# A conv-FFN kernel in split fp32: operand stores close behind their split, on another engine's queue, and operands of the second half loaded a group ahead

## The chip, the cores and the metric

The kernel runs on one core of one Trainium2 chip. The metric is the device time of one execution in microseconds; the time before is the median of three runs, 2267.11 us (2266.05 to 2268.96). The core has a tensor engine (PE; its weight loads are listed as PEld), a vector engine (DVE), a scalar engine (ACT), a general engine (POOL) and a synchronisation engine (SP), each with an instruction queue of its own that runs in order. A DMA is issued by an instruction in one of these queues: while that instruction waits for its data, everything behind it in the queue waits too.

## The reference, cut to what matters

One layer (S = 2048 tokens, D = 1024, F = 2816): a gated linear attention mixer, and then a feed-forward block with a causal convolution over the tokens.

```python
h = rmsnorm(x, mix_norm_w)
x = x + gla_mixer(h, ...)            # q, k, v, r, gates; scan over chunks; @ w_out
h = rmsnorm(x, ffn_norm_w)
u = causal_dwconv(h @ w_up, conv_w, conv_b)      # 3 taps over the tokens
g, val = jnp.split(u, 2, axis=-1)
x = x + (jax.nn.silu(g) * val) @ w_down
return rmsnorm(x, final_norm_w)
```

## The kernel before

**Products.** All large products are done in fp32 by three passes: `split` writes the rounded high half of an operand on ScalarE (a cast, L183) and the low half, what is left, on VectorE (a subtraction, L184); `mm3p` (L176 to L178) then issues high x low, low x high and high x high into one accumulation. On top of that, 2 x 2 blocks are multiplied with seven products, named p1, p5, p6, p7, p4, p2 and p3 in the order in which they run. p1, p6, p7 and p4 of a column add up in one PSUM bank (`ua`), and after p1, p6 and p7 ScalarE copies its contents out (c1 and c2 at L1050, c3 at L1145) before the next of the four may write on. p5 and p3 share the bank `uc`; p2 has its own, `ub`.

**Stages.** The mixer is done in four passes over the token tiles, R, A, B and Y. Y adds w_out's product to x; the result x1 goes to DRAM (`x1d`, L742), is normalised (`rows`), and is transposed and scaled into the operand rows of the feed-forward block (`blocks`, L745 to L762). Of those, the tiles of the first 1024 tokens stay on the chip (`hb2`); those of the second 1024 go to DRAM (`h2f`, L762) through a ring of two tiles. Then `phase_u(s)` runs for the halves s = 0 and s = 1: eleven groups g of two columns f, and in each group 14 jobs (seven products times two columns; a job is 12 matmuls 512 wide, four contraction tiles in three passes). A group multiplies the operands h (`hop`, kept on the chip, 4 x 512 columns in high and low) with the columns of w_up, convolves, gates (`gated`: silu(g) * val, on VectorE), and stores the seven combinations of its result that the down projection needs (`ad`, L1079 to L1095): three straight from the product, four over tiles that POOL adds up (`as`). The down projection follows after s = 1.

**Operands h.** The seven operands of each quarter of a half (`prep_h2`: p1, p5, p7, p3, p6, p2, p4 in its own order) are made from the rows, split into a tile `h2p` (L183 and L184), and stored to DRAM (`hd`, L785); four quarters make a half. This is spread over time by `spread`: a step each Y1 = 2.8 us of the planner's clock in pass Y for the first half, and each U1 = 11 us in phase U of s = 0 for the second half, starting U0 = 20 us in. A step first issues the store of the step before (`store()` at its head), so the operands of a step are in `held` for a whole step. The first half has three h2p tiles in the ring, the second half one. `load_op(s, o)` (L846) brings operand o of half s back in four DMAs, one for a quarter, into `uh`, where each product has exactly one tile: the load for s = 1 overwrites the operand of s = 0, so it waits until PE has used that for the last time. It is issued for s = 1 at the jobs k = 0, 2, ... 12 of s = 1's first group.

**Order.** Instructions are written in the order of a planner's clock: every `mm3p` advances it by 0.227 us a matmul, and `later_do(us, fn)` puts work off until the clock has gone that much further. The framework then sets each engine's order from this, and resolves what waits for what. Weights of a column come in two halves (`ur_f_0`, `ur_f_1`, L1017, two DMAs each, on SP except in the first group), into a ring of four, a group ahead; POOL forms the sums that p5, p6 and p3 need (`us`, L1027 to L1045). The DMAs that SP issues therefore stand in one row: weight loads, `ad` stores, operand stores, row loads (L780) and operand loads.

## Time and profile before

| | |
|---|---|
| median of three runs | 2267.11 us |
| profiled execution, its own time | 2264.65 us |
| its span | 2262.9 us |
| granted TensorE clock, mean | 0.983 |
| last x1 store of pass Y issued | 944.1 us |
| phase U, s = 0, groups g0 to g10 | 918.6 to 1401.1 us |
| preparation of the second half's operands | 960.2 to 1273.6 us |
| phase U, s = 1 | from 1401.1 us |

The page gives busy times of the engines, the DMA queues, the chain of work that ended last, and groups of instructions. The number behind a stage in a table of windows is the time in which each engine was busy in it; the granted clock is the share of full speed that the throttle allowed. In lists of waits, an engine's idle time is put down to what ended it. The rows on which the prediction rests are shown there.

### The profile page before, as it was taken

The numbers are of one execution on the slowest core, as the hardware profiler recorded it, in microseconds if no ns is written. First come the engines' busy times: TensorE is split into PE (matmuls) and PEld (weight loads), VectorE is DVE, ScalarE is ACT, GpSimd is POOL, SyncE is SP. The second block draws the span as 40 slices with busy tenths as digits, with TensorE's granted clock in tenths as the row PEclk, the third lists the DMA queues.
The fourth block names the chain that finished last, engine by engine and source line by source line (L and its number), as shares of the span: only waits on it lengthen the run. The fifth ranks groups of instructions, "written<-read, shape, count | busy, mean of one in ns | idle before, by whom it ended". The sixth has DMA issues, their size and how long they took to land.

```text
span 2262.9 us, 29154 instructions
## 1 busy us (share of the span) xinstructions
PE 2132.6 (94%) x9948; PEld 1744.8 (77%) x9948; DVE 1612.6 (71%) x2175; ACT 1109.8 (49%) x2020; POOL 698.5 (31%) x602
## 2 busy tenths in 40 slices
PE   5999989989997998889989999899999999999998
PEld 3888778877886886767777788788888888888886
DVE  7755787788778764388778777577777786557554
ACT  4554755565556675444454444344454543332343
POOL 1000111111111000254545565455555544035100
PEclk9999999999999999999999999999999999999999
DMA  6545684368457798934543437624233368454443
GB/s 220 191 163 182 215 280 133 124 207 307 158 162 232 265 330 307 327 125 139 171 146 126 140 98 258 209 73 124 86 117 94 112 229 324 136 186 158 140 166 118
DMA packets 301045, 411.77 MB, mean 182 GB/s; under 512 B 23246, under 2 KB 159614, under 8 KB 300896
## 3 DMA queue, kind: packets, MB, share of 16 engines
q1 hardware_dynamic: 270476, 362.45, 47.9%
q10 hardware_dynamic: 30420, 47.46, 6.4%
q8 instruction: 78, 1.28, 0.2%
q14 instruction: 71, 0.58, 0.1%
HBM read 266.70 MB, written 143.13 MB: 181 GB/s over the span
## 4 chain that ended last, share of the span: by engine, by line
PE 65%; DVE 12%; DMA 10%; ACT 5%; issue 4%; POOL 3%; SPq 1%; ACTq 0%; DVEq 0%; POOLq 0%
PE ua L176 5%; PE ua L177 5%; PE ua L178 5%; PE pd_p L177 5%; PE pd_p L178 5%; PE pd_p L176 5%; PE uc L178 3%; PE uc L176 3%; PE uc L177 3%; PE mp_R L176 2%; DVE t L1068 2%; PE mp_R L177 2%; PE mp_R L178 2%; PE mp_Y L176 2%; DMA hd_p<-h2p_p 2%
## 5 line engine op out<-in xcount | busy, mean ns | idle before, releaser
L176 PE MATMUL ua<-h_p,uw_p 128*128 128x512 f32 x704 | 284.3, 404 | 42.5 <-ACT c L1145 31.9
L177 PE MATMUL ua<-h_p,uw_p 128*128 128x512 f32 x704 | 282.3, 401 | 0.0
L178 PE MATMUL ua<-h_p,uw_p 128*128 128x512 f32 x704 | 281.8, 400 | 0.0
L1068 DVE SCALAR_TENSOR_TENSOR t<-u,cw,t 128x1024 f32<-128x1024 f32 x176 | 250.9, 1427 | 13.2 <-ACT t L1066 12.4
L177 PE MATMUL pd_p<-dw_p,da 128*128 128x512 f32 x616 | 239.7, 389 | 0.8 <-DVE da L184 0.8
L176 PE MATMUL pd_p<-dw_p,da 128*128 128x512 f32 x616 | 239.6, 389 | 0.0
L178 PE MATMUL pd_p<-dw_p,da 128*128 128x512 f32 x616 | 239.6, 389 | 0.0
L184 DVE TENSOR_TENSOR uw_p<-ur,uw_p 128x512 fp32r<-128x512 f32 x176 | 162.9, 940 | 64.8 <-ACT uw_p L183 56.8
L184 DVE TENSOR_TENSOR da<-da_p,da 128x512 fp32r<-128x512 f32 x154 | 135.4, 932 | 98.9 <-ACT da L183 98.8
L176 PEld LDWEIGHTS ua<-h_p,uw_p 128*128 128x128 f32 x704 | 136.2, 194 | 77.0 <-ACT c L1145 35.3
L183 ACT CAST da<-da_p 128x512 fp32r<-128x512 f32 x154 | 85.2, 619 | 201.7 <-PE pd_p L178 147.5
L178 PEld LDWEIGHTS ua<-h_p,uw_p 128*128 128x128 f32 x704 | 136.2, 194 | 30.9
L177 PEld LDWEIGHTS ua<-h_p,uw_p 128*128 128x128 f32 x704 | 136.7, 194 | 30.2
L184 DVE TENSOR_TENSOR uw_p<-us,uw_p 128x512 fp32r<-128x512 f32 x132 | 119.1, 909 | 56.5 <-ACT uw_p L183 55.2
L183 ACT CAST uw_p<-us 128x512 fp32r<-128x512 f32 x132 | 82.1, 622 | 137.2 <-POOL us L1030 87.4
L176 PE MATMUL uc<-h_p,uw_p 128*128 128x512 f32 x352 | 138.1, 392 | 0.0
L178 PE MATMUL uc<-h_p,uw_p 128*128 128x512 f32 x352 | 138.0, 392 | 0.0
L177 PE MATMUL uc<-h_p,uw_p 128*128 128x512 f32 x352 | 138.0, 392 | 0.0
L1066 ACT ACTIVATE t<-u,cw 128x1024 f32<-128x1024 f32 x88 | 109.7, 1247 | 53.8 <-DVE u L1158 53.8
L177 PEld LDWEIGHTS pd_p<-dw_p,da 128*128 128x128 f32 x616 | 115.6, 188 | 25.2 <-DVE da L184 1.3
L176 PEld LDWEIGHTS pd_p<-dw_p,da 128*128 128x128 f32 x616 | 115.6, 188 | 24.2
L178 PEld LDWEIGHTS pd_p<-dw_p,da 128*128 128x128 f32 x616 | 115.6, 188 | 23.8
(251 smaller groups left out, 5427.5 us busy)
## 6 DMA issues: line engine op xcount, KB each, us to landing
ur<-in_ffn_w_up_dram SPq DMA_DIRECT2D x168, 256.0 KB, 3.4
da_p<-ad_p SPq DMA_DIRECT2D x154, 256.0 KB, 3.8
hd_p<-h2p_p SPq DMA_DIRECT2D x56, 512.0 KB, 3.2
h_p<-hd_p SPq DMA_DIRECT2D x56, 512.0 KB, 7.6
ad_p<-as_p SPq DMA_DIRECT2D x88, 256.0 KB, 2.2
ad_p<-t SPq DMA_DIRECT2D x66, 256.0 KB, 3.2
x<-in_x_dram SPq DMA_DIRECT2D x32, 512.0 KB, 4.8
ch<-in_ffn_w_down_dram SPq DMA_DIRECT2D x61, 256.0 KB, 4.8
```

The source lines that it names most:

```text
L176: nc.tensor.matmul(ps_ap, ah, bl, start=(first and i == 0), stop=False, **kw)
L177: nc.tensor.matmul(ps_ap, al, bh, start=False, stop=False, **kw)
L178: nc.tensor.matmul(ps_ap, ah, bh, start=False, stop=(last and i == len(pairs) - 1), **kw)
L183: nc.scalar.copy(hi, src)
L184: nc.vector.tensor_sub(lo, src, f32(hi))
L1066: nc.scalar.activation(t, u[:, 2:2 + TS], AF.Identity, scale=cw[:, 2, c:c + 1], bias=cw[:, 3, c:c + 1])
L1068: nc.vector.scalar_tensor_tensor(t, u[:, k:k + TS], cw[:, k, c:c + 1], t, op0=ALU.mult, op1=ALU.add)
```

## The change

Six edits, all in where and when DMAs are issued:

- the rows of the second half go to DRAM from `cp_tile`, the ring of four that the evictions c1 and c2 use, instead of a ring of two of their own;
- the first half's h2p ring is four tiles instead of three;
- a step's operand store is issued `HLY` = 1.5 us (first half) or 3.0 us (second half) of the planner's clock behind its split, not at the head of the next step, and the second half's on ScalarE's queue;
- the x1 stores of the last two tiles are on ScalarE's queue;
- the second half's preparation starts 14 us into phase U, not 20;
- operand o of s = 1 is loaded in the last group of s = 0, directly behind the second column's job of the same product, and not in s = 1's first group.

```diff
-    Y0, Y1, U0, U1 = 3.0, 2.8, 20.0, 11.0
+    Y0, Y1, U0, U1 = 3.0, 2.8, 14.0, 11.0
+    HLY = (1.5, 3.0)
...
-               lambda name: p.tile([P, 2, 512], F32R, tag="h2p", name=name, bufs=3))
+               lambda name: p.tile([P, 2, 512], F32R, tag="h2p", name=name, bufs=4))
...
-        nc.sync.dma_start(x1d[t], xt)
+        (nc.scalar if t + 2 >= NTT else nc.sync).dma_start(x1d[t], xt)
...
-            t = hb2_tile(f"hb2_{tt}_{k}", tt < TT)
+            t = hb2_tile(f"hb2_{tt}_{k}") if tt < TT else cp_tile(f"hb3_{tt}_{k}")
...
-    def hb2_tile(name, kept):
-        return yp["p"].tile([P, 512], F32, tag="hb2" if kept else "hb3", name=name, bufs=10 if kept else 2)
+    def hb2_tile(name):
+        return yp["p"].tile([P, 512], F32, tag="hb2", name=name, bufs=10)
...
                 o, hl = held.pop()
-                nc.sync.dma_start(hd[s, o, j], f32(hl))
+                (nc.scalar if s else nc.sync).dma_start(hd[s, o, j], f32(hl))
...
             held.append((o, hl))
+            later_do(HLY[s], store)
...
-            if s > 0 and k == 0:
-                need(*(f"h2p{jj}" for jj in range(PAIRS, 2 * PAIRS)))
-            if s > 0 and k < 2 * len(OPS) and k % 2 == 0:
-                load_op(s, OPS[k // 2])
...
+            if s + 1 < NS and g == NQ - 1 and f % 2 == 1:
+                need(*(f"h2p{jj}" for jj in range(PAIRS, 2 * PAIRS)))
+                load_op(s + 1, o)
+            if o == "p3":
```

Line numbers of the changed kernel are one or two higher from L183 on (L184 is the cast, L786 the operand store, L848 the operand load, L1019 the weight load, L1052 and L1143 the evictions).

Three places show how the rows move. The first is ScalarE at products p6 and p7 of the group of columns 8 and 9 (s = 0). `uw` are weight halves being cast, `c_0_8` and `c_0_9` the evictions, `h2p` the operand step. Before:

```order
L183 CAST uw_9_p_11081<-ur_9_1_10818 128x512
L183 CAST uw_8_p_11098<-ur_8_1_10815 128x512
L1050 COPY c_0_8_11096<-ua_8_11003 128x512
L183 CAST uw_9_p_11115<-ur_9_1_10818 128x512
L1050 COPY c_0_9_11113<-ua_9_11022 128x512
L183 CAST uw_8_p_11146<-us_8_10907 128x512
L1145 COPY c_0_8_11135<-ua_8_11003 128x512
L183 CAST uw_9_p_11166<-us_9_10933 128x512
L183 CAST h2p_p_11453<-h2r_0_11433 128x512
L1145 COPY c_0_9_11161<-ua_9_11022 128x512
```

and now:

```order
L184 CAST uw_8_p_11103<-ur_8_1_10821 128x512
L786 DMA hd_p_2_328<-h2p_p_11596 128x1024
L1052 COPY c_0_8_11101<-ua_8_11008 128x512
L184 CAST uw_9_p_11121<-ur_9_1_10824 128x512
L184 CAST h2p_p_11718<-h2r_2_11402 128x512
L786 DMA hd_p_2_340<-h2p_p_11718 128x1024
L1052 COPY c_0_9_11119<-ua_9_11027 128x512
L184 CAST uw_8_p_11147<-us_8_10913 128x512
L1143 COPY c_0_8_11136<-ua_8_11008 128x512
L184 CAST uw_9_p_11167<-us_9_10934 128x512
L184 CAST h2p_p_11801<-h2r_0_11398 128x512
L786 DMA hd_p_2_324<-h2p_p_11801 128x1024
```

Three operand stores stand among the evictions where none stood, two of them directly ahead of a c2, and two casts of h2p steps stand here that stood elsewhere in the group.

The second is SP's queue at the boundary of the halves, where `ur_0` to `ur_3` are weights of s = 1, `ad_p_9` and `ad_p_10` stores of the last two groups of s = 0, and h_p<-hd_p the operand loads for s = 1. Before:

```order
L1017 DMA ur_0_0_13198<-in_ffn_w_up_dram 128x4x128 x2
L1079 DMA ad_p_9_351<-t_18_12880 512x1x128
L846 DMA h_p_13210<-hd_p_0_314 128x2x512
L1017 DMA ur_1_0_13201<-in_ffn_w_up_dram 128x4x128 x2
L1082 DMA ad_p_9_406<-t_19_12906 512x1x128
L1083 DMA ad_p_9_395<-t_19_12906 512x1x128
L1095 DMA ad_p_9_362<-as_9_p_12914 128x512
L1095 DMA ad_p_9_373<-as_9_p_12917 128x512
L1095 DMA ad_p_9_417<-as_9_p_12920 128x512
L1095 DMA ad_p_9_384<-as_9_p_12923 128x512
L1017 DMA ur_0_1_13204<-in_ffn_w_up_dram 128x4x128 x2
L1017 DMA ur_1_1_13207<-in_ffn_w_up_dram 128x4x128 x2
```

and now, one group later in the program:

```order
L848 DMA h_p_13206<-hd_p_2_340 128x2x512
L848 DMA h_p_13206<-hd_p_3_341 128x2x512
L1084 DMA ad_p_10_407<-t_21_13213 512x1x128
L1085 DMA ad_p_10_396<-t_21_13213 512x1x128
L1097 DMA ad_p_10_363<-as_10_p_13221 128x512
L1097 DMA ad_p_10_374<-as_10_p_13224 128x512
L1097 DMA ad_p_10_418<-as_10_p_13227 128x512
L1097 DMA ad_p_10_385<-as_10_p_13230 128x512
L1019 DMA ur_1_0_13236<-in_ffn_w_up_dram 128x4x128 x2
L1019 DMA ur_0_1_13239<-in_ffn_w_up_dram 128x4x128 x2
L1019 DMA ur_1_1_13242<-in_ffn_w_up_dram 128x4x128 x2
L1019 DMA ur_2_0_13305<-in_ffn_w_up_dram 128x4x128 x2
```

The weights ur_1_0, ur_0_1 and ur_1_1 stood ahead of group 9's last stores or right behind them, and stand now behind those of group 10 and behind the 28 operand loads; only ur_0_0 has kept its place.

The third is ScalarE at the end of pass Y, where x_14 and x_15 are the last two x1 tiles, and hb_14 rows on their way to DRAM. Now:

```order
L743 DMA x1d_92<-x_14_9221 128x1024
L203 ACTIVATE h_14_9613,ssq_d_9614<-x_14_9221 128x1024
L184 CAST uw_1_p_9676<-us_1_9674 128x512
L746 ACTIVATE h_14_9613<-x_14_9221,rstd_d_9618 128x1024
L743 DMA x1d_93<-x_15_9223 128x1024
L203 ACTIVATE h_15_9640,ssq_d_9641<-x_15_9223 128x1024
L1052 COPY c_0_0_9672<-ua_0_9659 128x512
L746 ACTIVATE h_15_9640<-x_15_9223,rstd_d_9645 128x1024
L759 ACTIVATE hb_14_0_9688<-pt_d_0_9683,nw_506 128x128 x4
```

Before, the two x1 stores stood on SP's queue, among the operand loads of s = 0:

```order
L846 DMA h_p_9606<-hd_p_3_309 128x2x512
L742 DMA x1d_92<-x_14_9221 128x1024
L846 DMA h_p_9633<-hd_p_0_310 128x2x512
L846 DMA h_p_9633<-hd_p_1_311 128x2x512
L846 DMA h_p_9633<-hd_p_2_312 128x2x512
L846 DMA h_p_9633<-hd_p_3_313 128x2x512
L742 DMA x1d_93<-x_15_9223 128x1024
```

Both have moved from behind those loads to just behind the sums that make their tiles.

## Prediction

> **What bounds the kernel now.** I read the page first, then a table of windows by stage, then the waits in those windows, and last the timeline around one stall. The page:

> ```profile
> span 2262.9 us, 29154 instructions
> PE 2132.6 (94%) x9948; PEld 1744.8 (77%) x9948; DVE 1612.6 (71%) x2175; ACT 1109.8 (49%) x2020; POOL 698.5 (31%) x602
> ```

> TensorE is busy 94% of the span, so what the change can win is idle time of PE, and the slow clock behind it. The windows (start:end, length, then busy time of PE, PEld, DVE, ACT, POOL, then granted clock, DMA share, GB/s) show where that is: the end of pass Y, gate/value groups g0 (from 918.6), g1 (from 972), g2 to g7, then g8 to g10, and s = 1's g0.

> ```profile
> 840.00:918.60 78.60, 68.52 (x306) 54.95 (x305) 38.03 (x63) 43.79 (x97) 9.26 (x11) 0.96 0.92 318
> 972.00:1018.00 46.00, 38.61 (x153) 30.57 (x153) 38.73 (x39) 22.73 (x36) 24.20 (x22) 0.93 0.44 143
> 1018.00:1285.80 267.80, 242.36 (x1002) 195.23 (x1001) 213.72 (x216) 125.02 (x191) 132.69 (x120) 0.95 0.44 144
> 1285.80:1401.10 115.30, 115.30 (x504) 94.22 (x503) 84.56 (x91) 57.00 (x85) 73.71 (x61) 1.00 0.51 163
> 1401.10:1449.30 48.20, 42.31 (x172) 34.05 (x171) 29.43 (x32) 19.15 (x29) 22.37 (x19) 0.93 0.71 244
> ```

> In g8 to g10, where the preparation of the second half is over, PE has no gap: 115.3/3 = 38.4 us a group, 2.74 a job of its 14. With the preparation a group takes 267.8/6 = 44.6. Against 38.4, g1 loses 7.6 and g2 to g7 lose 37.2, **44.8 us** together. s = 1's first group loses 48.2 - 38.4 = **9.8**. At the end of Y PE is idle 10.1 of 78.6 us.

> The waits of 972 to 1286 (who, for whom, total, times, longest) say what the 44.8 is:

> ```profile
> ACT h2p_p L183 <- DMA hd_p<-h2p_p: 56.1, 19, 8.3
> PE ua L176 <- ACT c L1145: 28.2, 7, 5.2
> ```

> and the timeline of one of them (start, duration, engine, line; in brackets the idle time before) shows it link by link, SP and ACT and PE:

> ```profile
> 1075.63 5.43 SPq L1095 DMA_DIRECT2D ad_p<-as_p  x4
> 1081.15 2.09 SPq L1017 DMA_DIRECT2D ur<-in_ffn_w_up_dram  x4
> 1083.29 0.49 SPq L785 DMA_DIRECT2D hd_p<-h2p_p  x1
> 1089.73 0.62 ACT L183 CAST h2p_p<-h2r 128x512 fp32r<-128x512 f32 x1 [8.29 <-DMA hd_p<-h2p_p]
> 1090.26 0.58 ACT L1145 COPY c<-ua 128x512 f32<-128x512 f32 x1
> 1090.89 0.79 PE L176 MATMUL ua<-h_p,uw_p 128*128 128x512 f32 x1 [5.20 <-ACT c L1145]
> ```

> The operand store waits on SP's queue behind four ad stores and four weight loads, the next cast waits on ScalarE until that store has landed (one h2p tile), the eviction of p7 stands behind the cast, and p4 waits 5.20 us for it. After it the clock drops (windows of PE's timeline, the granted clock third from the end, and the two matmuls that ended shorter stalls in pass Y):

> ```profile
> 1091.00:1094.00 3.00, 3.00 (x8) 2.38 (x9) 2.44 (x5) 2.50 (x4) 0.58 (x1) 0.52 0.68 223
> 853.61 0.50 PE L176 MATMUL mp_Y<-w_Y_p,h_Y_p 128*128 128x512 f32 x1 [2.58 <-ACT h_Y_p L183]
> 853.50:857.00 3.50, 3.16 (x9) 2.29 (x10) 2.58 (x4) 2.20 (x7) 0.00 (x0) 0.71 0.73 215
> 857.00:860.00 3.00, 3.00 (x12) 2.41 (x11) 0.34 (x1) 0.34 (x1) 0.00 (x0) 0.77 1.05 410
> 878.57 0.50 PE L176 MATMUL mp_Y<-w_Y_p,h_Y_p 128*128 128x512 f32 x1 [1.70 <-ACT h_Y_p L183]
> 878.50:881.00 2.50, 2.21 (x8) 1.61 (x9) 2.14 (x4) 2.14 (x7) 0.00 (x0) 1.00 0.56 151
> ```

> Three us at 0.52 cost about 1.5. The two windows from 853.5 follow a stall of 2.58 us, and lose (1 - 0.71) x 3.5 + (1 - 0.77) x 3 = 1.7; the stall of 1.70 lost nothing.

> **Term A, the end of Y.** Rows to DRAM from a ring of four, x1 stores of the last two tiles on ScalarE. The waits of 840 to 960:

> ```profile
> ACT hb L758 <- DMA h2f<-hb: 8.2, 2, 5.1
> PE mp_Y L176 <- ACT h_Y_p L183: 8.4, 3, 4.1
> ACT uw_p L183 <- DMA x1d<-x: 10.1, 1, 10.1
> PE ua L176 <- ACT c L1145: 3.8, 1, 3.8
> ```

> ScalarE waits twice for the ring of two; of PE's three waits for the operand rows, 8.4 - 1.7 = 6.7 us come from that. It waits 10.1 us for an x1 store that SP issued only behind the h_p loads, and PE 3.8 of it. With 1.7 of clock behind each of three stalls the whole is 6.7 + 3.8 + 5.1 = 15.6. But the DMA engines are 0.92 busy in 840:918.6: the h_p loads of s = 0 go at their pace, and PE that comes earlier waits for them. The larger ring also is one that g0's first evictions use, so those now wait for a row store. I count half of the ring's part (6.7 + 3.4)/2 = 5 and two thirds of the x1 part (3.8 + 1.7), 3.6: **-8.6**. Bounds: -3.8 (the x1 wait alone) and -15.6.

> **Term B, stores on ScalarE's queue behind their split.** SP's part of the stall goes: the store no longer waits for ad stores and weights. Its cost is the issue on ScalarE, 0.33 us as the h2f store takes there, 28 times, beside an engine busy 125.02 of 267.8; nothing unless something waits. What it brings is a wait: the store needs the low half, which VectorE subtracts late, and ScalarE queues behind it.

> In the timeline of ScalarE, VectorE and POOL, and among the page's DMA issues:

> ```profile
> 935.32 0.33 ACTq L762 DMA_DIRECT2D h2f<-hb  x1
> 1106.26 0.39 PE L176 MATMUL ua<-h_p,uw_p 128*128 128x512 f32 x1
> 1108.57 0.62 ACT L183 CAST h2p_p<-h2r 128x512 fp32r<-128x512 f32 x1 [0.38 <-DMA hd_p<-h2p_p]
> 1090.39 0.69 DVE L184 TENSOR_TENSOR h2p_p<-h2r,h2p_p 128x512 fp32r<-128x512 f32 x1 [7.32 <-ACT h2p_p L183]
> 1119.14 1.79 DVE L184 TENSOR_TENSOR h2p_p<-h2r,h2p_p 128x512 fp32r<-128x512 f32 x1
> 1120.85 3.48 DVE L184 TENSOR_TENSOR uw_p<-ur,uw_p 128x512 fp32r<-128x512 f32 x2
> 1118.70 1.67 POOL L1089 TENSOR_TENSOR as_p<-t,t 128x512 f32<-128x512 f32 x1 [1.18 <-DVE t L1075]
> hd_p<-h2p_p SPq DMA_DIRECT2D x56, 512.0 KB, 3.2
> ```

> The cast of 1108.57 had its subtraction end only at 1120.93: VectorE was busy with the convolution and the gating product, then took 1.74 to 1.79 a subtraction beside POOL's adds. By the order of the changed kernel such a store stands right ahead of the c copies of p6, twice or three times a group. p6 f0's copy must be over when p6 f1 is (16.5 us into the group). g4 began at 1106.26 (its first ua matmul), so the subtraction above ended 14.7 into it, and the last of the four that run beside the adds about 18.1 to 19.8. A store that waits for one of the middle ones, plus 0.3 of issue and 0.6 of copy, lets the copy end at 15.6 to 19: a stall of 0 to 2.5, I take 1.3. The second store of the row: its cast waits until the first has landed (3.2), then 0.6 + 0.7 + 0.3 + 0.6 for cast, subtraction, issue and copy, 5.4 after the first store, where PE gives 0.9 + 2.74 = 3.6: 1.8 us more. So a group keeps 1.3 + 1.8 = 3.1, too short each for the clock; seven groups (the last step now falls in g6, the first in g0) keep about 21 of 44.8: **-24**. Bounds: -44.8, all gone, and +5, ScalarE held for ten us as in the row above with little taken away.

> If both stalls of a group run together into 3.0 us, the clock behind them costs 1.7 more by the 853.5 rows, 12 us in seven groups, and the sum would be 2257; I count them apart. [...]

> VectorE does not bind yet: 213.72/6 = 35.6 us a group against 38.4.

> **Term C, second-half operands loaded in g10.** Before, they cost 9.8 us in s = 1's g0:

> ```profile
> PE ua L176 <- DMA h_p<-hd_p: 5.9, 1, 5.9
> 1411.97 1.68 POOL L1089 TENSOR_TENSOR as_p<-t,t 128x512 f32<-128x512 f32 x1 [1.19 <-DVE t L1075]
> 1413.68 5.10 SPq L1095 DMA_DIRECT2D ad_p<-as_p  x4
> 1418.83 2.68 SPq L1017 DMA_DIRECT2D ur<-in_ffn_w_up_dram  x5
> ur<-in_ffn_w_up_dram SPq DMA_DIRECT2D x168, 256.0 KB, 3.4
> ```

> All 28 loads now stand on SP ahead of g10's last stores, each behind PE's use of the old operand, and with them go the weights: in the order of the changed kernel s = 1's ur_1_0, ur_0_1 and ur_1_1 come behind the four as stores of group 10; only ur_0_0 is ahead. Before, all four were ahead. PE's second job of s = 1 needs ur_1_0. By the rows, the last as store leaves at 1418.8, 17.7 us after g10's end (1401.1); then 0.4 of issue, 3.4 to landing, 0.6 cast, 0.7 subtraction: 22.8 after the end, where PE wants it at 2.74. That is 20 us; I take off 2 since VectorE and POOL have no weights of s = 1 to prepare meanwhile: 18, plus 2.5 of clock, 20.5 lost. Net of the 9.8 saved: **+10.7**. Bounds: +5 (the chain 3 us shorter still, no clock) and +13.5 (20 + 3.4 - 9.8).

> The other edits (first-half ring of four, its stores 1.5 us behind the split, on SP) act where SP was not what PE waited for: nothing, beyond A's bounds.

> **Sum.** -8.6 - 24 + 10.7 = -21.9. The profiled execution took 2264.65 us, so 2242.8; the median shown is 2.46 higher, 2267.11: forecast **2245**.

> **The rivals.**
> 1. The wait moves whole to ScalarE (slower). The cast of 1108.57 against its subtraction at 1120.93 speaks for it, the step of 1089.73 and 1090.39, subtracted at once, against it. If each group keeps its 6.4 and A gives only 3.8: -3.8 + 10.7 = +6.9, **2274**. It turns to slower once A and B together bring less than 10.7 - 4.5 = 6.2 us.
> 2. The weights come in time at the half: if what the order shows is without effect because the as stores leave early, C is -7 (the 9.8 less one job of 2.74) in place of +10.7: **2227**. Against it: POOL's adds begin 10.9 us after the end, and SP issues the four stores over 5.10.
> 3. The stalls of B go almost whole, since with the jam gone VectorE's subtraction comes sooner: -8.6 - 40 + 10.7 = -38, **2229**. For it: the step at 1090.39; against it: the product and the adds stay where they are in the group.
> 4. The edit does not do what it says, for the second half still has one h2p tile: each cast still waits for a landing of 3.2, and VectorE, at 35.6 of 38.4 in a shorter group, is late by half a job (1.4) more: a group keeps 4.5, B is 44.8 - 31.5 = -13, **2256**; with the joined stalls of above 2257.

> **Chances.** Forecast (2236 to 2250) 0.50; rival 1 0.12; rival 2 0.08; rival 3 0.15; rival 4 0.15. The range reaches over rivals 2 to 4: 2225 to 2264, with rival 1 and some tail left out. A measurement of this kernel can tell about 0.2%, 4.5 us, from no change: faster (below 2262.6) 0.82, within 0.07 (the upper edge of rival 4, the lower of rival 1), slower 0.11.

> **What would show it.** A: no wait of ACT hb L759 for h2f at 850 to 905, none for x1d near 942, and new ones of c L1052 for h2f in g0. B: no ACT wait of 8 us for hd; waits of ACT's own queue for DVE h2p at 2 to 10 us; groups g1 to g6 near 41.4. C: PE idle 15 to 20 us a job after s = 1 begins, ended by the cast of uw from ur_1_0, then groups of 38.4. Wrong if groups stay at 44 (rival 1), if PE runs on at the half (rival 2), or if g2 to g6 fall to 38.4 (rival 3).

## The result, and the profile after

The changed kernel took 2254.45 us (median of four, 2252.84 to 2255.93) against 2267.13 for the kernel before (four, 2266.05 to 2268.96): ratio 0.9943, 95% interval 0.9926 to 0.9960, 12.7 us faster. The profiled execution of the changed kernel took 2255.93, its span is 2254.2. Its page, in the two lines that were shown of before:

```profile
span 2254.2 us, 29125 instructions
PE 2125.4 (94%) x9948; PEld 1738.4 (77%) x9948; DVE 1609.5 (71%) x2175; ACT 1111.0 (49%) x2020; POOL 712.1 (32%) x602
```

PE runs the same matmuls in the same stages, so the stages can be cut at the same matmul in both traces. The windows of the changed kernel, in the columns of the prediction: the end of Y, g1, g2 to g7, g8 to g10, and s = 1's g0.

```profile
840.80:909.90 69.10, 64.90 (x304) 52.20 (x304) 37.60 (x62) 43.27 (x97) 6.23 (x8) 1.00 0.97 341
961.73:1008.88 47.15, 37.63 (x153) 29.99 (x152) 40.00 (x39) 21.89 (x34) 25.24 (x22) 0.89 0.42 139
1008.88:1258.36 249.48, 235.74 (x1002) 188.63 (x1001) 213.31 (x216) 125.09 (x190) 144.61 (x120) 0.99 0.47 154
1258.36:1373.58 115.22, 115.22 (x503) 94.16 (x502) 83.71 (x87) 54.54 (x80) 62.13 (x54) 1.00 0.49 159
1373.58:1437.61 64.03, 42.00 (x173) 33.54 (x171) 34.94 (x36) 22.48 (x34) 31.19 (x25) 0.81 0.57 190
```

| stage, cut at the same matmuls | before | after | difference |
|---|---|---|---|
| end of Y | 78.6 | 69.4 | -9.2 |
| g0 | 53.5 | 51.9 | -1.6 |
| g1 | 46.1 | 47.2 | +1.1 |
| g2 to g7 | 267.8 | 249.5 | -18.3 |
| g8 to g10 | 115.2 | 115.2 | 0.0 |
| s = 1, g0 | 48.2 | 64.0 | +15.8 |
| from there to the last matmul | 804.7 | 807.7 | +3.0 |

By the terms of the prediction: A -10.8, B -17.2, C +15.8, in sum -12.2, close to the 12.7 between the medians. The 3.0 at the end of this one execution is mostly a single stall of the down projection, where nothing was changed: near 1901 us PE waits 1.9 us for a subtraction of VectorE (`da`) and then runs 3.4 us at half clock. In the kernel before that wait is 0.8 us, in e1 1.1, in e5 3.6.

The differences are right, since both traces are cut at the same matmuls, but the stages called g1 and g2 to g7 here and in the prediction are not whole groups. A group is 14 jobs of 12 matmuls, 168, and the row of g1 counts 153 (with those that lie across an edge). Cut at every 168th matmul of the phase, with a whole group without a gap (g8) at 38.56 us:

| whole groups | before | lost | after | lost |
|---|---|---|---|---|
| g1 | 49.7 (from 966.15) | 11.1 | 50.8 (from 955.84) | 12.2 |
| g2 to g7 | 269.6 (from 1015.84) | 38.2 | 251.3 (from 1006.62) | 19.9 |

So the preparation cost 49.3 us before, not the 44.8 of the prediction, and costs 32.1 now.

The waits of 962 to 1258 answer to those shown of before:

```profile
ACT h2p_p L184 <- DMA hd_p<-h2p_p: 29.2, 17, 3.3
PE ua L177 <- ACT c L1052: 21.6, 9, 8.3
ACT c L1052 <- DVE h2p_p L185: 12.2, 6, 3.8
PE ua L177 <- ACT c L1143: 1.6, 3, 0.9
```

ScalarE's wait for operand stores to land fell from 56.1 to 29.2 us, PE's wait for c3 from 28.2 to 1.6. A wait that did not exist stands in their place: the copy of c1 and c2 behind a store that waits for VectorE, 12.2 us on ScalarE, and PE waits 21.6 for those copies (4.7 before). The worst is in g1. ScalarE, VectorE and PE there:

```profile
962.77 0.62 ACT L184 CAST h2p_p<-h2r 128x512 fp32r<-128x512 f32 x1 [0.67 <-DVE h2r L791]
969.16 1.21 DVE L1077 TENSOR_TENSOR t<-t,t 128x1024 f32<-128x1024 f32 x1
972.09 0.68 DVE L185 TENSOR_TENSOR h2p_p<-h2r,h2p_p 128x512 fp32r<-128x512 f32 x1
972.85 0.33 ACTq L786 DMA_DIRECT2D hd_p<-h2p_p  x1
977.18 0.62 ACT L184 CAST h2p_p<-h2r 128x512 fp32r<-128x512 f32 x1 [3.29 <-DMA hd_p<-h2p_p]
981.23 0.33 ACTq L786 DMA_DIRECT2D hd_p<-h2p_p  x1
981.60 0.58 ACT L1052 COPY c<-ua 128x512 f32<-128x512 f32 x1 [3.80 <-DVE h2p_p L185]
982.24 0.80 PE L177 MATMUL ua<-h_p,uw_p 128*128 128x512 f32 x1 [8.35 <-ACT c L1052]
```

Read from the top: the subtraction comes 9.3 us behind its cast, since VectorE does convolution and gating products first (L1077 is one); the store follows; the next cast waits until it has landed; its own store waits for VectorE again; then the copy of c2; and PE has stood for 8.35 us.

At the boundary of the halves (PE, ScalarE, POOL's adds of group 10, SP):

```profile
1382.34 1.26 POOL L1091 TENSOR_TENSOR as_p<-t,t 128x512 f32<-128x512 f32 x1 [2.09 <-DVE t L1077]
1386.24 1.26 POOL L1095 TENSOR_TENSOR as_p<-t 128x512 f32<-128x512 f32 x1
1379.40 4.49 SPq L848 DMA_DIRECT2D h_p<-hd_p  x4
1387.08 3.96 SPq L1097 DMA_DIRECT2D ad_p<-as_p  x4
1391.64 6.09 SPq L1019 DMA_DIRECT2D ur<-in_ffn_w_up_dram  x6
1397.82 0.62 ACT L184 CAST uw_p<-ur 128x512 fp32r<-128x512 f32 x1 [16.82 <-DMA ur<-in_ffn_w_up_dram]
1398.49 0.79 PE L177 MATMUL ua<-h_p,uw_p 128*128 128x512 f32 x1 [22.03 <-ACT uw_p L184]
```

The weights of the second job leave SP behind the as stores of group 10, as its order has it, and PE waits 22.03 us for them.

### The profile page after: what moved, and what is told of

It reads as the page before. It is cut to its first block, busy times and chain, and to the rows that moved or that the text cites. A ratio compares the mean times of both kernels' runs of the same rounds, so it can differ in the third digit from the quotient of the medians.

```text
span 2254.2 us, 29125 instructions
## 1 busy us (share of the span) xinstructions
PE 2125.4 (94%) x9948; PEld 1738.4 (77%) x9948; DVE 1609.5 (71%) x2175; ACT 1111.0 (49%) x2020; POOL 712.1 (32%) x602
## 3 DMA queue, kind: packets, MB, share of 16 engines
q1 hardware_dynamic: 266156, 346.72, 46.1%
## 4 chain that ended last, share of the span: by engine, by line
PE 67%; DVE 12%; DMA 9%; issue 5%; ACT 4%; POOL 3%; ACTq 0%; SPq 0%; DVEq 0%; POOLq 0%
PE ua L177 5%; PE ua L178 5%; PE ua L179 5%; PE pd_p L178 5%; PE pd_p L177 5%; PE pd_p L179 5%; PE uc L178 3%; PE uc L179 3%; PE uc L177 3%; DVE t L1070 2%; PE mp_R L177 2%; PE mp_R L178 2%; PE mp_R L179 2%; PE mp_Y L177 2%; PE mp_Y L178 2%
## 5 line engine op out<-in xcount | busy, mean ns | idle before, releaser
L177 PE MATMUL ua<-h_p,uw_p 128*128 128x512 f32 x704 | 281.2, 399 | 45.3 <-ACT uw_p L184 22.0
L178 PE MATMUL ua<-h_p,uw_p 128*128 128x512 f32 x704 | 279.2, 397 | 0.0
L179 PE MATMUL ua<-h_p,uw_p 128*128 128x512 f32 x704 | 278.5, 396 | 0.0
L177 PEld LDWEIGHTS ua<-h_p,uw_p 128*128 128x128 f32 x704 | 134.2, 191 | 81.3 <-ACT c L1052 26.5
L184 ACT CAST da<-da_p 128x512 fp32r<-128x512 f32 x154 | 85.1, 619 | 204.5 <-PE pd_p L179 148.7
L179 PEld LDWEIGHTS ua<-h_p,uw_p 128*128 128x128 f32 x704 | 134.3, 191 | 30.1
L178 PEld LDWEIGHTS ua<-h_p,uw_p 128*128 128x128 f32 x704 | 134.3, 191 | 29.6 <-DVE uw_p L185 0.4
L184 ACT CAST uw_p<-us 128x512 fp32r<-128x512 f32 x132 | 82.1, 622 | 126.7 <-POOL us L1032 74.2
## 6 DMA issues: line engine op xcount, KB each, us to landing
ur<-in_ffn_w_up_dram SPq DMA_DIRECT2D x168, 256.0 KB, 3.5
da_p<-ad_p SPq DMA_DIRECT2D x154, 256.0 KB, 3.8
h_p<-hd_p SPq DMA_DIRECT2D x56, 512.0 KB, 9.2
ad_p<-as_p SPq DMA_DIRECT2D x88, 256.0 KB, 2.3
ad_p<-t SPq DMA_DIRECT2D x66, 256.0 KB, 3.0
x<-in_x_dram SPq DMA_DIRECT2D x32, 512.0 KB, 5.1
ch<-in_ffn_w_down_dram SPq DMA_DIRECT2D x61, 256.0 KB, 4.3
hr_A_p<-h1d_p SPq DMA_DIRECT2D x56, 256.0 KB, 2.9
```

The source lines that it names most:

```text
L177: nc.tensor.matmul(ps_ap, ah, bl, start=(first and i == 0), stop=False, **kw)
L178: nc.tensor.matmul(ps_ap, al, bh, start=False, stop=False, **kw)
L179: nc.tensor.matmul(ps_ap, ah, bh, start=False, stop=(last and i == len(pairs) - 1), **kw)
L184: nc.scalar.copy(hi, src)
```

## Experiments

**e1: the weights of s = 1's first group from within group 10.** Every other group's weights are loaded a group ahead; this does the same across the halves.

```diff
-        load(0, 0)
-        load(0, 1)
+        if s == 0:
+            load(0, 0)
+            load(0, 1)
...
+            if k % (2 * len(OPS)) in (2, 7) and g + 1 == NQ and s + 1 < NS:
+                load(0, int(k % (2 * len(OPS)) == 7), s + 1, up.setdefault(s + 1, {}))
```

> The changed kernel, with the weights of s = 1's first group loaded from within group 10 of s = 0 (as every other group's are a group ahead), so that ur_1_0, ur_0_1 and ur_1_1 stand among the operand loads and ahead of group 10's as stores. Theory (the 22.2 us stall and 2.1 us of slow clock at the boundary come from weights queued behind those stores): it goes nearly whole, 24 us less than the changed kernel, 2228 to 2236. Rival (the 28 operand loads on SP or the DMA engines make the weights late, wherever they stand): a stall of 10 us or more stays, 2240 to 2252.

Measured: 2235.54 us, ratio to before 0.9873 (0.9841 to 0.9904), 18.9 below the changed kernel. SP and s = 1's g0 in its trace:

```profile
1354.85 7.07 SPq L848 DMA_DIRECT2D h_p<-hd_p  x8
1362.44 7.32 SPq L1022 DMA_DIRECT2D ur<-in_ffn_w_up_dram  x4
1369.85 11.90 SPq L848 DMA_DIRECT2D h_p<-hd_p  x12
1372.90:1415.40 42.50, 40.05 (x173) 31.87 (x172) 33.76 (x28) 20.05 (x30) 28.02 (x20) 1.00 0.88 293
```

The last four weight loads leave SP 10 us ahead of s = 1, among the operand loads; its g0 takes 42.5 in place of 64.0, less than the 48.2 of before too. The rival, that 28 operand loads make the weights late wherever these stand, falls. The median gained less than g0 did, 18.9 for 21.5: in the group behind it PE has two new stalls for evictions, of 1.3 and 0.9 us.

**e2: rows and x1 alone, on the kernel before.**

```diff
-        nc.sync.dma_start(x1d[t], xt)
+        (nc.scalar if t + 2 >= NTT else nc.sync).dma_start(x1d[t], xt)
...
-            t = hb2_tile(f"hb2_{tt}_{k}", tt < TT)
+            t = hb2_tile(f"hb2_{tt}_{k}", True) if tt < TT else cp_tile(f"hb3_{tt}_{k}")
```

> The kernel before, with the ring of four for the rows and the two x1 stores on ScalarE alone. Theory (this is the whole of the 11 us won by the middle of g0): 2256, 11 below the kernel before, and all of it still there at the end. Rival (the earlier operand stores of the first half, 1.5 us behind their split, won a part): 3 to 7 us.

Measured: 2254.22, ratio 0.9949 (0.9931 to 0.9967); by stage, the end of Y 70.7 and g0 49.4, 12.0 less than before, g2 to g7 267.5 and s = 1's g0 48.9, as before. This is the whole of term A; the earlier stores of the first half add nothing to it that these times show (in e3, which changes nothing there, the two stages together differ by 2.4 us from the kernel before). Rows and x1 stores were moved together, so how the gain is shared between them is not shown. The new wait that the ring of four was to bring is there, and small (first row); the second row is what is left of the 8.2 us on the rows:

```profile
ACT c L1050 <- DMA h2f<-hb: 3.7, 1, 3.7
ACT hb L758 <- DMA h2f<-hb: 3.6, 1, 3.6
```

**e3: the operand loads in group 10 alone, on the kernel before.** The two removed and the three added lines of the change at `load_op`, nothing else.

> The kernel before, with the operand loads of s = 1 issued in group 10 alone. Theory: the 9 us of stall and slow clock before go, 24 come in their place: 15 to 16 slower, 2283. Rival (the cost is a meeting of this with the stores on ScalarE): no slower than 5 us, 2265 to 2272.

Measured: 2282.01, ratio 1.0070 (1.0046 to 1.0095), 16 slower; s = 1's g0 takes 63.6. So this edit alone costs what it costs in the changed kernel, with no store on ScalarE anywhere.

**e4: the changed kernel with the second half's operand stores on SP.**

```diff
-                (nc.scalar if s else nc.sync).dma_start(hd[s, o, j], f32(hl))
+                nc.sync.dma_start(hd[s, o, j], f32(hl))
```

> The changed kernel with the second half's operand stores on SP's queue, still 3.0 us behind their split. Theory A (the queue is what counts: on SP the store stands behind ad stores and weights again): groups g1 to g6 go back to about 44.6, 10 to 17 us slower than the changed kernel. Theory B (only the distance from the split counts): within 4 us of the changed kernel. Theory C (a wait for VectorE costs more on ScalarE than on SP): faster by more than 4 us.

Measured: 2266.09, ratio 1.0005 (0.9990 to 1.0021), 11.6 above the changed kernel. The waits in its g1 to g7:

```profile
ACT h2p_p L184 <- DMA hd_p<-h2p_p: 58.7, 17, 10.3
PE ua L177 <- ACT c L1143: 24.4, 6, 7.1
SPq L786 <- DVE h2p_p L185: 121.3, 19, 13.1
```

With the store still 3 us of the planner's clock behind its split, the waits of before are back, 58.7 and 24.4 us for 56.1 and 28.2, and g2 to g7 take 264.9. Most of the stores are not late: SP has come to them first and waits for VectorE (third row). But five stores, one a group, stand behind the four as stores and two weight loads as they did before. One of them, and the subtraction that makes its tile:

```profile
1114.51 1.79 DVE L185 TENSOR_TENSOR h2p_p<-h2r,h2p_p 128x512 fp32r<-128x512 f32 x1
1121.30 1.86 SPq L1019 DMA_DIRECT2D ur<-in_ffn_w_up_dram  x2
1123.21 0.50 SPq L786 DMA_DIRECT2D hd_p<-h2p_p  x1
```

It leaves 6.9 us after its subtraction has ended; on ScalarE's queue no store left more than 0.1 us after. Theory A holds, and theory B, that only the distance counts, falls. No run changes the distance alone, so what that is worth on ScalarE's queue is not shown.

**e5: e1 with the preparation starting at 20.**

```diff
-    Y0, Y1, U0, U1 = 3.0, 2.8, 14.0, 11.0
+    Y0, Y1, U0, U1 = 3.0, 2.8, 20.0, 11.0
```

> The kernel e1 (weights of s = 1 loaded in group 10) with the preparation starting at 20 again in place of 14. What is left of the preparation's stalls is 24 us, 8.5 + 2.9 of it one stall at 972, where the second step's subtraction ends 9 us behind its cast and the eviction of p6 stands behind the store. Theory (that stall comes from where the steps fall in g1): it shrinks by half or more, and one more group is touched, -2 to -6 against e1. Rival (any phase meets VectorE's backlog): within 3 us of e1.

Measured: 2229.37, ratio 0.9838 (0.9808 to 0.9868), the fastest of all. Its g1 takes 43.6 for e1's 46.7, g2 to g7 248.7 for 249.6. PE's longest wait for c copies goes from 8.3 to 3.9 us, while the landing waits stay:

```profile
ACT h2p_p L184 <- DMA hd_p<-h2p_p: 28.6, 17, 3.4
PE ua L177 <- ACT c L1055: 15.6, 10, 3.9
```

The intervals of e5 and e1 overlap, so the gain over e1 is shown by the trace of g1 and not by the times.

**e10: the changed kernel with the start at 20 alone.** The same line on the changed kernel.

> The changed kernel with the preparation starting at 20 in place of 14 and nothing else. Theory (the start of 14 sets g1's stall of 8.5 and 2.3 us): that stall falls to about 4 and 3, the boundary's 22 us stay, 2248 to 2252. Rival (e5's gain over e1 was not the start): 2253 to 2256, and a stall of 8 us in g1.

Measured: 2251.88, ratio 0.9945 (0.9927 to 0.9962): at the upper edge of the theory's range by its median, and not told apart from the changed kernel's 0.9943 by its ratio. Its trace sides with the theory: g1 43.5 for 47.2, g2 to g7 247.9 for 249.5, a stall of 3.94 where 8.35 stood.

**e7: e1 with the second half's stores on GpSimd.** The line of e4 with `nc.gpsimd` for `nc.scalar`.

> The kernel e1 with the second half's stores on GpSimd's queue, so that GpSimd and no longer ScalarE waits for the low half. Theory (the stalls left are ScalarE's wait for VectorE): they fall from 24 us to 8 to 12, 12 to 16 below e1. Rival 1 (they are the landing before the next cast, with one h2p tile, 29.2 us of ScalarE's waits): within 5 us of e1. Rival 2 (GpSimd's sums of weights and its adds now queue behind stores): slower than e1 by 5 to 15 us.

Measured: 2261.85, ratio 0.9975 (0.9959 to 0.9992), 26 above e1. The waits:

```profile
ACT h2p_p L184 <- DMA hd_p<-h2p_p: 82.6, 17, 10.9
POOL hd_p L786 <- DVE h2p_p L185: 54.0, 14, 6.4
PE ua L177 <- ACT c L1055: 42.8, 7, 9.1
```

All three expectations miss the size, and rival 2 names the sign. ScalarE no longer waits for VectorE, but the store now stands in an engine that itself waits for VectorE (54.0 us at the stores alone), behind its adds and copies, and it leaves later, up to 4.5 us after its subtraction has ended; ScalarE then waits for its landing, 82.6 us with one h2p tile.

**e8: e1 with two h2p tiles, three t tiles.**

```diff
-            t = pools["us"].tile([P, TS], F32, tag="t", name=f"t_{s}_{c}", bufs=4)
+            t = pools["us"].tile([P, TS], F32, tag="t", name=f"t_{s}_{c}", bufs=3)
...
-                       lambda name: wx_.tile([P, 2, 512], F32R, tag="h2p", name=name, bufs=1))
+                       lambda name: wx_.tile([P, 2, 512], F32R, tag="h2p", name=name, bufs=2))
```

> The kernel e1 with two h2p tiles in the second half; the convolution's ring t has three tiles in place of four to make room. Theory (the landing before the next cast is most of what is left): the stalls left fall from 24 us to 8 to 12, 12 to 16 below e1. Rival 1 (the wait for VectorE's subtraction is): within 5 us of e1. Rival 2 (three t tiles are too few): stalls in every group of both halves, slower by 10 us or more.

Measured: 2255.95, ratio 0.9953 (0.9936 to 0.9969). Rival 2 holds for s = 1, which is 26 us longer in the trace than in e1; in s = 0, g1 to g7 take 293.8 for 296.3. What of that is the second tile and what the smaller t ring this run can't tell. Hence e9.

**e9: e5 with two h2p tiles, room from the weight tiles.** `WX = 2` for 3, t at four tiles, two h2p tiles as in e8.

> The kernel e5 (weights in group 10, start at 20) with two h2p tiles in the second half, the room taken from the extra weight tiles (two in place of three), all four t tiles kept. In e8 the landing waits fell from 28 to 12 us, PE's waits for p6's eviction from 19.7 to 18.2 only, and s = 1 lost 27 us to the three t tiles. Theory (the stalls left are VectorE's late subtraction with the store ahead of the eviction, not the landing): s = 0's groups within 4 us of e5, and s = 1 unchanged. Rival (the landing was the rest, and e8's t ring hid it): s = 0 8 to 14 us shorter than in e5. Rival 2 (six weight tiles are too few): stalls in s = 1's groups, slower than e5.

Measured: 2240.58, ratio 0.9893 (0.9872 to 0.9915), slower than e5. In s = 0 g1 takes 48.4 and g2 to g7 248.9, against 43.6 and 248.7. The waits:

```profile
ACT h2p_p L184 <- DMA hd_p<-h2p_p: 10.1, 6, 3.8
PE ua L177 <- ACT c L1055: 18.8, 6, 5.3
```

The landing waits fell from 28.6 to 10.1 us, PE's wait rose from 15.6 to 18.8. The rival's 8 to 14 us did not come; the theory's bound of 4 us is missed by one, and six weight tiles also cost something (s = 1's g0 is 47.9 against 42.2). But the run does not separate the landing from the rest, for with two tiles the steps also follow each other faster: the last 27 casts run from 957.4 to 1114.8 us, in e5 from 966.2 to 1196.8. They fall into four groups in place of six: g1 to g4 have stalls of 3.5 to 5.3 us, longer than in e5, and g5 to g7 none. What a second tile would bring at the old pace stays open.

## Why the prediction was right, and where it was off

**The direction and the three mechanisms** were right, each shown by an edit of its own: A by e2, C by e3 and e1, the queue in B by e4. The time, 2254.45, lies above the 2236 to 2250 to which the forecast itself gave 0.50, and inside the range laid over the rivals. Rival 1 (the wait moves whole to ScalarE), rival 2 (the weights come in time) and rival 3 (the stalls go whole) did not happen. Rival 4 came nearest, in time (2256) and in what a group keeps: 4.5 by its account, 32.1/7 = 4.6 by whole groups. Of its two steps, the landing of the one h2p tile does stand in the chain of several stalls, as below, and e9 does not rule it out; the other, VectorE late by half a job everywhere, is not what the groups show, which keep from 0 (g7) to 12.2 us (g1).

**A, forecast -8.6, measured -10.8** (e2: -12.0). That the DMA engines would hold back half of the ring's gain was too cautious: they went from 0.92 to 0.97 busy in the window and the end of Y got 9.2 us shorter. Against the full 15.6 stands a longer wait in g0 that the sum did not have: PE stands 3.0 us for the normalised rows of `h` (L746), 1.2 before. Of the two waits for h2f, 8.2 us, 2.9 stayed on the rows and 3.4 came anew on an eviction in the changed kernel.

**B, forecast -24, measured -17.2.** Both stalls of the forecast are there. In g4 ScalarE and PE show the second, a store whose cast first waits for a landing:

```profile
1112.74 0.62 ACT L184 CAST h2p_p<-h2r 128x512 fp32r<-128x512 f32 x1 [2.09 <-DMA hd_p<-h2p_p]
1114.80 0.33 ACTq L786 DMA_DIRECT2D hd_p<-h2p_p  x1
1115.17 0.58 ACT L1052 COPY c<-ua 128x512 f32<-128x512 f32 x1 [1.80 <-DVE h2p_p L185]
1115.81 0.50 PE L177 MATMUL ua<-h_p,uw_p 128*128 128x512 f32 x1 [2.56 <-ACT c L1052]
```

This kind is 2.56, 2.61 and 1.27 us long in g4, g5 and g6 (forecast 1.8); a late subtraction alone makes 2.94 in g3 and 0.80 in g4 (forecast 1.3); 1.58 in g2 follows a cast that waited for VectorE's row sums.

Two terms were mis-sized. The 44.8 that the preparation cost before was 49.3 by whole groups. And seven groups were to keep 3.1 each, 21.7: they kept 32.1, of which g1 alone has 12.2. That g2 to g7 keep 19.9, or 3.3 a group, looks like the forecast and is partly luck, since g7 keeps nothing, g2 to g6 keep 1.6 to 6.3, and the stalls of 2.94 and 2.56 us each brought 3.4 us at half clock, which the sum had at nothing.

g1 is the larger miss. The step that failed took the two stalls of a group from a subtraction that runs in the window of POOL's adds. In g1, by the rows above, it waited out the convolution behind 9.3 us of other VectorE work, landing, the next cast and the next subtraction followed in a row, and all of it lay ahead of one copy. With the start at 20 (e5, e10) the whole group g1 takes 47.2 and 47.1 in place of 50.8. So the new start time, for which the sum has no term, cost about 4 us: shown in two traces, not separable in the medians.

The move to another engine's queue did not take the landing away: 2.6 to 4.6 us on ScalarE's queue in the changed kernel, 2.6 to 6.3 on SP's in the kernel before. What it changed is how long a store stands behind other work: 6.9 us after its subtraction in the rows of e4, at most 0.1 on ScalarE's queue. ScalarE's queue in place of SP's was worth 11.6 us (e4), and GpSimd's in place of ScalarE's cost 26 (e7).

**C, forecast +10.7, measured +15.8** (e3: +15.4 in the same stage). The order was read rightly; the stall was 22.0 us where the sum had 18. Two terms were off: the 2 us taken off because VectorE and POOL would be less loaded, and the landing. They were less loaded: POOL's adds took 1.26 us each in place of 1.29 to 1.75, and began 8.8 us after the boundary, not 10.9. But the DMA engines were full, with 28 operand loads of 512 KB issued from 1343 on. The windows and the DMA issues of 1385 to 1399:

```profile
1385.00:1399.00 14.00, 0.51 (x1) 0.29 (x1) 0.53 (x1) 0.62 (x1) 2.48 (x2) 0.50 1.09 369
ur<-in_ffn_w_up_dram SPq DMA_DIRECT2D x6, 256.0 KB, 6.0
```

With DMA share at 1.09, weights took 6.0 us to land in place of the 3.4 of the page, four stores after adds that had ended at 1387.5 left SP only by 1391.0, and the last operand loads took 4.49 us to issue four. I had priced a transfer of a crowded moment with the median of the whole program.

**Sum.** A brought 2.2 us more than forecast, B 6.8 less, and C cost 5.1 more: 9.7 above 2245, 2254.7, where 2254.45 was measured. That it comes out so close is chance: the stages are those of two single executions, 8.7 us apart in span, where the medians are 12.7 apart.

## What to carry to other kernels

In these runs a DMA's instruction cost what stood behind it in its queue while it waited: on ScalarE the copies of c1 and c2 stood 12.2 us behind stores that waited for VectorE. Put it in the queue whose next work can bear that wait, and judge the queue by its own waits, not by its idle share (GpSimd was 32% busy in the changed kernel, and the worst of the three tried: e7 took 26 us more than e1). Where loads are pulled ahead, look at what they now stand in front of: PE waited for none of the 28 loads at the boundary (5.9 us before), and 22.0 us for the weights behind them. When a transfer falls into a burst, take its landing time from a burst: here 6.0 us, where the page had 3.4.

The version that came out best, e5, is the change with two corrections, the weights of s = 1 loaded a group ahead and the old start of 20: 0.9838 of before against 0.9943.

## What the runs showed of the hardware

Two stalls of the same length do not cost the same. In e1 and e8, PE resumed after 2.89 and 2.87 us. Each stall, and the granted clock (third from the end) in the windows of 3.41 us over which its idle time falls and behind them:

```profile
1066.14 0.79 PE L177 MATMUL ua<-h_p,uw_p 128*128 128x512 f32 x1 [2.89 <-ACT c L1055]
1061.97:1065.38 3.41, 1.28 (x6) 0.71 (x4) 2.57 (x3) 0.40 (x1) 2.96 (x2) 1.00 1.06 309
1065.38:1068.79 3.41, 2.65 (x6) 2.15 (x7) 2.07 (x2) 1.71 (x4) 3.33 (x3) 0.50 0.91 352
1068.79:1072.21 3.42, 3.42 (x9) 2.63 (x8) 2.13 (x3) 1.74 (x5) 0.36 (x1) 0.50 0.64 212
1020.26 0.50 PE L177 MATMUL ua<-h_p,uw_p 128*128 128x512 f32 x1 [2.87 <-ACT c L1055]
1015.31:1018.73 3.42, 2.08 (x10) 1.38 (x8) 3.42 (x5) 0.05 (x1) 1.17 (x1) 1.00 0.76 269
1018.73:1022.14 3.41, 1.88 (x8) 1.56 (x9) 3.41 (x5) 3.41 (x5) 0.49 (x1) 1.00 0.62 193
1022.14:1025.55 3.41, 3.41 (x17) 2.72 (x16) 3.18 (x5) 2.29 (x6) 0.00 (x0) 1.00 1.02 305
```

Cut by that grid, the two traces have 20 windows at full clock in which PE was idle for 1.91 us or more, and each was followed by one at 0.50; of the 848 with 1.87 us or less none was. A window at 0.50 was followed by one at full clock where PE was idle for 0.44 us or less in it (20 times), and by another at 0.50 where it was idle for 0.61 or more (17 times). So in these two traces a stall that filled at least 1.91 us of one window was paid for, all twelve of 3.8 us or more among them, and the single one of 1.70 us in the prediction's rows was free. Between the two the length alone did not tell: in the changed kernel the 2.56 us of g4 were followed by 3.41 us at 0.50, and the 2.61 of g5, 1.20 in one window and 1.41 in the next, were not.
